# A hybrid decoder block on Trainium2: the seven-product scheme taken to the pooling and gate projections, with the stages in another order

## The chip, the cores and the metric

The kernel runs on one core of a Trainium2 chip. The metric is device time in microseconds, the median of several executions; lower is better. The engines are called as the profile calls them: PE (TensorE, the matmuls), PEld (its weight loads), ACT (ScalarE), DVE (VectorE), POOL (GpSimd) and SP (SyncE, which issues most loads).

## The reference, cut to what matters

528 tokens (16 learned meta tokens and 512 real ones) of width 1024 pass through one block:

```python
hn = rmsnorm(h, norm1_g)
q, k, v, glr, r, u, ga, gb = split(hn @ w_in)
o = rmsnorm(gla_chunked(q, k, v, log_a), gla_norm_g)      # 4 heads, chunked
y_a = (o * silu(r)) @ w_a
pooled = multiscale_pool(u)          # trailing means over 2, 4, 8, 16 tokens, minus the token
y_b = (einsum(pooled, w_pool_grp) * pool_scale) @ w_b
gate_a = sigmoid(ga + b_gates[:D]); gate_b = sigmoid(gb + b_gates[D:])
h = h + (gate_a * y_a + gate_b * y_b) @ w_o
hn = rmsnorm(h, norm2_g)
a, bv = split(causal_dwconv(hn @ w_up))
h = h + (silu(a) * bv) @ w_down
return rmsnorm(h, final_norm_g)[N_META:]
```

## The kernel before

**Layout.** Channels lie on the 128 partitions and tokens along the free axis, so a projection of 1024 channels is 8 output blocks m, each summed over 8 input blocks k. An f32 product is made of three matmuls on rounded halves: high by high, high by low, low by high. A tile therefore comes as a pair such as `xh`, `xl`: ACT copies the high part, DVE subtracts it for the low part (`split`, L248). Tokens are cut in two column parts, since a PSUM bank holds 512 numbers: `TAIL` is 258 + 256 columns (from token 14), `FULL` is 264 + 264. One block m is then 8 x 3 x 2 = 48 matmuls, and a pair of blocks 96.

**Order of the work.** The stages follow each other on PE as they are written: norm 1; k, q, the decay gates; v; the chunked linear attention with the r projections between its chunks (`gla_back`, `gla_front`, `proj_r`, L461-467); the head norms over the whole length (`head_squares`, `head_norm`, L469-506); then u, ga, a, gb, grp, b, o in that order, eight blocks each (grp is small); then the up projections with the down projections between them; and the final norm.

**The first part, k to o.** The weights of one block m come as a 512 KB chunk, loaded by SP three chunks and more ahead. `prep_chunk` (L124) makes the high part on ACT (L133) and the low part on DVE (L134), two chunks ahead. Each block's sum lands in a `psum` tile; DVE scales it by the first norm's factor (`scaled`, L262). The normalisation is thus applied behind the product: `xh`, `xl` hold x times the gain g1, without the factor `rstd1`.

**The pooling.** All of u is projected first (L511). The window sums of the four channel groups g are doubling trees of shifted adds: one add for g = 0, four for g = 3. They run on POOL (L520-537). While ga is projected, `pool_split` (L539) takes the mean minus the token on DVE (L544) and splits it into `pah`, `pal`. The gate ga is passed through a sigmoid (L555), and the result of a is multiplied by it as it is evicted (L560).

**The up stage** works in units, each of one pair of output blocks, from 1 MB of weights. `fetch` (L640) loads a unit's raw tile two and three units ahead. For the first three of its four blocks, `make_low` (L671) writes minus the raw weight, rounded, with ACT, and POOL then issues three accumulating transfers that add the weight from memory once more, which leaves the low part `gl`. `make_high` (L681) makes `gh` on ACT. Units 0 to 3 are plain, 96 matmuls. Units 4 to 21 (`up_fast`, L797) use a scheme of seven block products where a 2 x 2 product of blocks has eight. It needs sums of weight blocks (L704, splits `sh_..`, `sl_..`) and combinations of input blocks, which `cross` (L769) makes once per four input blocks, on an input that is already normalised. A group is 12 matmuls of 258 columns, a unit 7 groups, 84 matmuls. The bank x takes three groups, q two, v and y one each. ACT evicts x after its first group (L805), q after its first (L808), x after its second (L811) and its third (L817); DVE combines (L813-819). The next group into a bank waits until ACT has read the last. The work of the next units stands on the engines between these evictions, and each engine takes its instructions strictly in the order in which they stand.

**What sets the buffers.** The first part's pools are closed behind o (`first.close()`, L616); then the unit pools open (`rawp` 3, `gp` 2, `unitp` 14, `ssp` 2, `t3p` 4, eight PSUM banks). At the end of o, `h2` is made with its squares: DVE adds (L603), ACT makes `h2h` and the square (L604, L607), POOL adds the squares up (L611). The sum's split `n2h`, `n2l` (L613) feeds the norm matmuls (L758), which stand in the first up unit behind its first 48 matmuls.

Of the kernel before, what the change touches and what calls it, by code (L numbers as in the profile page):

```python
# [32 lines left out]
UCOLS = (((12, 270), (270, L)), ((10, 270), (270, L)), ((6, 268), (268, L)), FULL)  # L33
H0 = 12
HALF = ((H0, 270), (270, L))
HN = 258
PLAIN = 4
LAG = 3
CROSS = {(0, 1): 0, (1, 0): 1, (1, 1): 2, (2, 0): 3}
PARTS = ((0, 6), (6, 6), (12, 6), (18, 4))  # L40
# [14 lines left out]
for _name, _n in (  # L55
    ("k", 4), ("q", 4), ("v", 8), ("r", 8), ("u", 8), ("ga", 8), ("a", 8),
    ("gb", 8), ("grp", 2), ("b", 8), ("o", 8),
):
    ORDER[_name] = _at
    _at += _n  # L60
NCHUNK = _at

# [6 lines left out]
def hybrid_block(ctx: ExitStack, tc: tile.TileContext, xt, g1d, wts, wup, wdown, wglr, wgk, vecs, out):  # L69
# [4 lines left out]
    lastp = ctx.enter_context(tc.tile_pool(name="lastp", bufs=12))  # L74
    first = ctx.enter_context(ExitStack())
    firstp = first.enter_context(tc.tile_pool(name="firstp", bufs=16))
    midp = first.enter_context(tc.tile_pool(name="midp", bufs=8))
    wrawp = first.enter_context(tc.tile_pool(name="wrawp", bufs=3))
    whlp = first.enter_context(tc.tile_pool(name="whlp", bufs=3))
    work = first.enter_context(tc.tile_pool(name="work", bufs=5))  # L80
    constf = first.enter_context(tc.tile_pool(name="constf", bufs=1))
# [6 lines left out]
    class Pairs:  # L88
# [12 lines left out]
        "xh": lastp, "xl": lastp, "r": lastp, "gb": lastp, "h2": lastp, "h2h": lastp, "h2l": lastp,  # L101
        "kq_mid": midp, "kq_far": midp, "zh": midp, "zl": midp, "mh": midp, "ml": midp,
    }

    def big(name, dt=F32):
        return Pairs(name, HOME.get(name, firstp), dt)
# [76 lines left out]
    g1 = constf.tile([P, KT], F32, tag="g1", name="g1")  # L183
# [212 lines left out]
    o = big("o")  # L396
# [34 lines left out]
    def gla_back(s):  # L431
# [26 lines left out]
        for h in range(4):  # L458
            act.activation(o.pair(h)[:, :, c : c + w], heads[:, 2 * h : 2 * h + 2, 0:w], AF.Copy)
# [3 lines left out]
    for s in range(4):  # L463
        gla_back(s)
        gla_front(s + 1)
        proj_r(s + 1)
    gla_back(4)

    def head_norm(h):  # L469
        so = column_sums(f"nos{h}", osp[2 * h], osp[2 * h + 1], TAIL)  # L470
        ro = osq[2 * h][:, T0:]
        done, _ = rsqrt_mean(osq[2 * h], so, TAIL, 256, osq[2 * h + 1])
        for e in range(2):
            m = 2 * h + e
            dve.scalar_tensor_tensor(o[m][:, T0:], o[m][:, T0:], v1("glag", e), ro, ALU.mult, ALU.mult)
        return done

    osq = big("osq")
    osp = big("osp", F32R)

    def head_squares(h):
        act.activation(osq.pair(h)[:, :, T0:], o.pair(h)[:, :, T0:], AF.Square)
        t = osq[2 * h][:, T0:]
        dve.tensor_tensor(t, t, osq[2 * h + 1][:, T0:], ALU.add)
        split(osp[2 * h][:, T0:], osp[2 * h + 1][:, T0:], t)

    head_squares(0)
    proj_r(5)
    head_squares(1)
    proj_r(6)  # L490
    head_norm(0)
    head_squares(2)
    proj_r(7)
    head_norm(1)
    head_squares(3)

    u = big("u")

    def proj_u(m):
        acc = project(f"pu{m}", ORDER["u"] + m, xh, xl, UCOLS[m // 2])  # L500
        scaled(u[m], acc, UCOLS[m // 2])

    proj_u(0)
    head_norm(2)
    proj_u(1)
    done = head_norm(3)
    zh, zl = big("zh", F32R), big("zl", F32R)
    with tc.issue_after(done.ins):
        for m in range(8):
            act.activation(r[m][:, T0:], r[m][:, T0:], AF.Silu)  # L510
    for m in range(2, 8):  # L511
        proj_u(m)
        for i in (2 * m - 4, 2 * m - 3) if m < 6 else ():
            dve.tensor_tensor(o[i][:, T0:], o[i][:, T0:], r[i][:, T0:], ALU.mult)
            split(zh[i][:, T0:], zl[i][:, T0:], o[i][:, T0:])

    pts = [big("pt0"), big("pt1")]
    pah, pal = big("pah", F32R), big("pal", F32R)
    curs = []
    for g in range(4):  # L520
        cur = u.pair(g)
        need = T0
        starts = []
        for i in reversed(range(g + 1)):
            starts.append(need)
            need = max(0, need - (1 << i))
        starts = starts[::-1]
        for i in range(g + 1):
            d = 1 << i
            nxt = pts[g % 2].pair(2 * (g // 2) + i % 2)  # L530
            a = starts[i]
            if a < d:
                pool.tensor_copy(nxt[:, :, a:d], cur[:, :, a:d])
                a = d
            pool.tensor_tensor(nxt[:, :, a:], cur[:, :, a:], cur[:, :, a - d : L - d], ALU.add)  # L535
            cur = nxt
        curs.append(cur)

    def pool_split(g):  # L539
        cur = curs[g]  # L540
        if g == 3:
            pool.tensor_scalar(cur[:, :, T0 : T0 + 1], cur[:, :, T0 : T0 + 1], 16.0 / (T0 + 1), None, ALU.mult)
        ug = u.pair(g)[:, :, T0:]
        dve.scalar_tensor_tensor(ug, cur[:, :, T0:], 1.0 / (2 << g), ug, ALU.mult, ALU.subtract)  # L544
        split(pah.pair(g)[:, :, T0:], pal.pair(g)[:, :, T0:], ug)

    ga = big("ga")
    for m in range(8):
        acc = project(f"pga{m}", ORDER["ga"] + m, xh, xl, TAIL)
        done = scaled(ga[m], acc, TAIL)  # L550
        if 3 <= m < 7:
            with tc.issue_after(done.ins):
                pool_split(m - 3)
    for m in range(8):
        act.activation(ga[m][:, T0:], ga[m][:, T0:], AF.Sigmoid, bias=v1("bga", m))  # L555

    for m in range(8):
        acc = project(f"pa{m}", ORDER["a"] + m, zh, zl, TAIL)
        for src, c in parts_of(acc, TAIL):
            dve.tensor_tensor(ga[m][:, c], src, ga[m][:, c], ALU.mult)  # L560

    gb = big("gb")
    for m in range(8):
        acc = project(f"pgb{m}", ORDER["gb"] + m, xh, xl, TAIL)
        scaled(gb[m], acc, TAIL)
    pbh, pbl = big("pbh", F32R), big("pbl", F32R)
    for m in range(8):
        hi, lo = chunk(ORDER["grp"] + m // 4)
        acc = ps(f"pgrp{m}")
        g = m // 2  # L570
        products(
            acc,
            [(hi[:, 2 * (m % 4) + k], lo[:, 2 * (m % 4) + k], pah[2 * g + k], pal[2 * g + k]) for k in range(2)],
            TAIL,
        )
        for src, c in parts_of(acc, TAIL):
            act.activation(pbh[m][:, c], src, AF.Copy, scale=v1("pscale", m))
            dve.scalar_tensor_tensor(pbl[m][:, c], src, v1("pscale", m), f32(pbh[m][:, c]), ALU.mult, ALU.subtract)

    for m in range(8):  # L580
        last = act.activation(gb[m][:, T0:], gb[m][:, T0:], AF.Sigmoid, bias=v1("bgb", m))
    table(LOG_EXP, last)

    mh, ml = big("mh", F32R), big("ml", F32R)
    for m in range(8):
        acc = project(f"pb{m}", ORDER["b"] + m, pbh, pbl, TAIL)
        t = gb[m][:, T0:]
        for src, c in parts_of(acc, TAIL):
            dve.tensor_tensor(gb[m][:, c], src, gb[m][:, c], ALU.mult)
        dve.tensor_tensor(t, t, ga[m][:, T0:], ALU.add)  # L590
        split(mh[m][:, T0:], ml[m][:, T0:], t)

    h2 = big("h2")
    for i in range(4):
        pool.memset(h2.pair(i)[:, :, H0:T0], 0.0)
        sp.dma_start(h2.pair(i)[:, :, T0:], xt[2 * i : 2 * i + 2, :, T0:].rearrange("k p t -> p k t"))
    h2h, h2l = big("h2h", F32R), big("h2l", F32R)
    tot = None
    for m in range(8):
        acc = project(f"po2{m}", ORDER["o"] + m, mh, ml, TAIL)  # L600
        t = h2[m][:, T0:]
        for src, c in parts_of(acc, TAIL):
            dve.tensor_tensor(h2[m][:, c], src, h2[m][:, c], ALU.add)  # L603
        act.activation(h2h[m][:, T0:], t, AF.Copy, scale=v1("g2", m))  # L604
        dve.scalar_tensor_tensor(h2l[m][:, T0:], t, v1("g2", m), f32(h2h[m][:, T0:]), ALU.mult, ALU.subtract)
        sq = wk(f"n2_sq{m}", TW)
        act.activation(sq, t, AF.Square)  # L607
        if tot is None:
            tot = sq
        else:  # L610
            pool.tensor_tensor(tot, tot, sq, ALU.add)  # L611
    sh, sl = wk("n2h", L, F32R), wk("n2l", L, F32R)
    split(sh[:, T0:], sl[:, T0:], tot)  # L613
    rstd2 = const.tile([P, L], F32, tag="rstd", name="rstd2")
    n2t = wk("n2t")
    first.close()  # L616

    def phase(name, bufs):
# [116 lines left out]
    def up_plain(n, i):  # L735
# [4 lines left out]
        for c in range(2):  # L740
# [21 lines left out]
            if (i, c) in CROSS:  # L762
                cross(CROSS[i, c])
# [222 lines left out]
```

## Time and profile before

| quantity | value |
|---|---|
| runs | 842.43, 843.38, 843.58 us; median 843.38 |
| profiled execution | 842.5 us, of which the span is 840.2 |
| busy PE / DVE / ACT / POOL | 824.1 / 548.8 / 420.7 / 117.2 us |
| matmuls | 6357 in the records |
| stages on the chain | v 61.9 to 108.2; attention, r, head norms to 187.1; u to 234.5; ga to 280.2; a to 325.8; gb to 371.4; grp to 382.9; b to 428.8; o to 474.8; up and down to 823 |
| granted PE clock | 1.00 in the stages |
| memory traffic | 98.40 MB, mean 117 GB/s |

How to read it: the profile is of one execution, which lies 0.9 us under the median of the runs. Busy times are per engine and overlap. The chain is followed back from the last instruction, each piece to what released it, and is shown in order of time; an engine that is off the chain has slack somewhere. A row of a timeline or of the chain starts with its start and its length in us. A row of a group gives its busy us and the mean ns of one instruction, then the engine's idle time ahead of them and what ended it. Ends of matmuls are modelled, so a matmul's length is longer than its spacing; the spacing is what counts, and it is taken from a stage's length divided by its count.

### The profile page before, as it was taken

The numbers are of one execution on the slowest core, as the hardware profiler recorded it, in microseconds if no ns is written. First come the engines' busy times: TensorE is split into PE (matmuls) and PEld (weight loads), VectorE is DVE, ScalarE is ACT, GpSimd is POOL, SyncE is SP. The second block draws the span as 40 slices with busy tenths as digits, with TensorE's granted clock in tenths as the row PEclk, the third lists the DMA queues.
The fourth block names the chain that finished last, engine by engine and source line by source line (L and its number), as shares of the span: only waits on it lengthen the run. The fifth ranks groups of instructions, "written<-read, shape, count | busy, mean of one in ns | idle before, by whom it ended". The sixth has DMA issues, their size and how long they took to land.

```text
span 840.2 us, 15052 instructions
## 1 busy us (share of the span) xinstructions
PE 824.1 (98%) x6357; PEld 796.1 (95%) x6357; DVE 548.8 (65%) x833; ACT 420.7 (50%) x606; POOL 117.2 (14%) x117
## 2 busy tenths in 40 slices
PE   8999999999999999999999999999999999999994
PEld 7999999999999999999999999999989989999883
DVE  6677344469846433346556288999659975899845
ACT  7287243266334311344245256886547844686542
POOL 4000000001750000000014121220122110320021
PEclk9999999999999999999999999999999999999998
DMA  7423221022332333262268045886547645775102
GB/s 242 131 68 106 80 76 51 26 76 76 101 101 78 100 101 92 85 201 96 82 218 234 1 101 115 179 169 184 147 126 156 155 126 165 152 172 141 51 25 100
DMA packets 31170, 98.40 MB, mean 117 GB/s; under 512 B 3488, under 2 KB 6304, under 8 KB 28288
## 3 DMA queue, kind: packets, MB, share of 16 engines
q1 hardware_dynamic: 20368, 79.10, 29.2%
q0 software_dynamic: 9504, 17.31, 12.6%
q8 instruction: 49, 0.80, 0.4%
q10 hardware_dynamic: 1232, 1.05, 0.4%
q14 instruction: 17, 0.14, 0.0%
HBM read 95.35 MB, written 2.10 MB: 116 GB/s over the span
## 4 chain that ended last, share of the span: by engine, by line
PE 94%; DVE 2%; DMA 2%; ACT 1%; issue 0%; SPq 0%; DVEq 0%; POOL 0%; ACTq 0%
PE pd L847 12%; PE x L791 9%; PE q L791 6%; PE pu L150 6%; PE pv L150 6%; PE po L150 5%; PE pb L150 5%; PE pr L150 5%; PE pgb L150 5%; PE pga L150 5%; PE pa L150 5%; PE pup L750 4%; PE y L791 3%; PE v L791 3%; PE pq L150 3%; PE pe L847 2%
## 5 line engine op out<-in xcount | busy, mean ns | idle before, releaser
L133 ACT ACTIVATE whi<-wraw 128x1024 fp32r<-128x1024 f32 (+2 forms) x78 | 78.9, 1014 | 202.0 <-PE pa L150 36.4
L134 DVE TENSOR_TENSOR wlo<-wraw,whi 128x1024 fp32r<-128x1024 f32 (+2 forms) x78 | 94.8, 1218 | 13.1 <-ACT whi L133 7.3
L679 POOL DMA_DIRECT2D gl<-in_wup_dram x66 | 59.2, 1220 | 292.3 <-ACT gl L677 251.8
L847 PE MATMUL pd<-g,gh 128*128 128x512 f32 (+1 forms) x304 | 93.1, 387 | 0.0
L847 PEld LDWEIGHTS pd<-g,gh 128*128 128x128 f32 x304 | 56.5, 188 | 12.0
L704 DVE TENSOR_TENSOR raw<-raw 128x512 f32<-128x512 f32 x72 | 49.5, 688 | 19.3 <-ACT gh L687 10.3
L847 PE MATMUL pd<-g,gl 128*128 128x512 f32 (+1 forms) x152 | 58.8, 387 | 0.0
L687 ACT ACTIVATE gh<-raw 128x1536 fp32r<-128x1536 f32 x22 | 32.7, 1484 | 27.6 <-PE pd L847 24.3
L535 POOL TENSOR_TENSOR pt<-u 128x1028 f32<-128x1028 f32 (+3 forms) x4 | 14.0, 3498 | 191.9 <-ACT whi L133 179.0
L832 ACT ACTIVATE cv<-z,vec 128x512 f32<-128x512 f32 x44 | 34.2, 812 | 1.1 <-DVE cv L834 1.1
L847 PEld LDWEIGHTS pd<-g,gl 128*128 128x128 f32 x152 | 28.5, 188 | 6.1
L677 ACT ACTIVATE gl<-raw 128x1536 fp32r<-128x1536 f32 x22 | 32.5, 1477 | 2.8 <-PE pd L847 2.2
L833 DVE SCALAR_TENSOR_TENSOR cv<-z,vec,cv 128x512 f32<-128x512 f32 x44 | 32.2, 745 | 0.0
L834 DVE SCALAR_TENSOR_TENSOR cv<-z,vec,cv 128x512 f32<-128x512 f32 x44 | 32.2, 745 | 0.0
L870 DVE TENSOR_TENSOR h<-pd,h 128x512 f32<-128x512 f32 x24 | 16.5, 687 | 24.0 <-PE pd L847 24.0
L250 DVE TENSOR_TENSOR gl<-raw,gh 128x1536 fp32r<-128x1536 f32 (+1 forms) x16 | 26.0, 1622 | 6.6 <-ACT gh L249 6.4
L249 ACT ACTIVATE gh<-raw 128x1536 fp32r<-128x1536 f32 (+1 forms) x16 | 22.0, 1376 | 11.7 <-PE pd L847 9.2
L150 PE MATMUL pr<-xh,whi 128*128 128x258 f32 (+1 forms) x128 | 26.1, 285 | 0.0
L150 PE MATMUL pv<-xh,wlo 128*128 128x264 f32 x128 | 26.0, 284 | 0.0
L150 PE MATMUL pu<-xh,wlo 128*128 128x258 f32 (+3 forms) x128 | 25.9, 284 | 0.0
L150 PE MATMUL pv<-xl,whi 128*128 128x264 f32 x128 | 25.9, 284 | 0.0
L150 PE MATMUL pu<-xh,whi 128*128 128x258 f32 (+3 forms) x128 | 25.9, 284 | 0.0
(822 smaller groups left out, 2780.0 us busy)
## 6 DMA issues: line engine op xcount, KB each, us to landing
wraw<-in_wts_dram SPq DMA_DIRECT2D x72, 512.0 KB, 3.6
raw<-in_wup_dram SPq DMA_DIRECT2D x22, 1024.0 KB, 5.8
gl<-in_wup_dram POOLq DMA_DIRECT2D x66, 256.0 KB, 7.4
raw<-in_wdown_dram SPq DMA_DIRECT2D x12, 768.0 KB, 4.4
h<-in_xt_dram SPq DMA_DIRECT2D x4, 514.0 KB, 5.8
raw<-in_wdown_dram SPq DMA_DIRECT2D x4, 512.0 KB, 3.5
x<-in_xt_dram SPq DMA_DIRECT2D x7, 264.0 KB, 6.0
out_dram<-h ACTq DMA_DIRECT2D x4, 256.0 KB, 2.4
```

The lines of the kernel that those rows point to most:

```text
L133: act.activation(hi[:, a:b], t[:, a:b], AF.Copy)
L134: dve.tensor_tensor(lo[:, a:b], t[:, a:b], f32(hi[:, a:b]), ALU.subtract)
L150: pe.matmul(acc[:, s, : b - a], w, x[:, a:b], start=(i == 0 and w is wh and x is xh), stop=(i == n - 1 and last),)
L677: act.activation(lo, loaded[n][:, 0:3], AF.Copy, scale=-1.0)
L679: pool.dma_start(lo[:, b], wup[i, :, b], accum_op=ALU.add)
L687: act.activation(hi, loaded[n][:, 0:3], AF.Copy)
L704: dve.tensor_tensor(raw[:, dst], raw[:, dst], raw[:, x], ALU.add)
L750: pe.matmul(acc[:, 0 : b - a], w[p], q[k][:, a:b], start=k == 0 and e == 0, stop=k == KT - 1 and e == 2,)
L791: pe.matmul(acc[:, 0:HN], w[a][:, block, k], x[k][b][:, at], start=first and k == 0 and e == 0, stop=k == 3 and e == 2, skip_group_check=n ...
L832: act.activation(cv, z[:, c, META:], AF.Identity, scale=v1("cw2", m), bias=v1("cb", m))
L833: dve.scalar_tensor_tensor(cv, z[:, c, META - 1 : L - 1], v1("cw1", m), cv, ALU.mult, ALU.add)
L847: pe.matmul(acc, w[p][:, c, k], gated[k0 + k][q][:, a:b], start=k == 0 and e == 0, stop=k == nk - 1 and e == 2,)
```

## The change

- **Seven products.** u, ga and gb become units of one pair each, on the same machinery as the up stage, from a weight array of 1 MB units (`wsq`). Eleven of the twelve pairs (u1 to u3, ga0 to ga3, gb0 to gb3) use the seven-product scheme at 264 columns; the first pair of u stays plain. Its input is x times g1 times `rstd1`: x is loaded again (`load_x`), and `cross_x` makes the normalised blocks and their combinations during u0 and a0 to a2.
- **Plain units.** a, grp, b and o become plain units as well, with the same `gl`, `gh` machinery in place of the chunks. The unit pools open behind the last r block; `unitp` has 11 buffers.
- **Order.** u0, a0, a1, a2, u1, u2, a3, u3, ga0 to ga3, gb0 to gb2, grp, b0, gb3, b1 to b3, o0 to o3, then up as before.
- **Pooling.** The trees are issued on DVE (`pool_tree`): for u0 behind a2, for u1 behind u1, for u2 behind a3, for u3 behind u3, each with the mean and the split.
- **Gates.** a is evicted by ACT and kept, and multiplied by the gate when that is there.
- **Head norms** are taken chunk by chunk inside the attention loop, on 4 heads by 128 tokens at once.

The program has 138 matmuls fewer: 11 x 12, and 6 of the head norms.

The diff, cut to the parts spoken of:

```diff
-    pts = [big("pt0"), big("pt1")]
-            pool.tensor_tensor(nxt[:, :, a:], cur[:, :, a:], cur[:, :, a - d : L - d], ALU.add)
...
+    seq = [("plain", "u", 0)] + [("plain", "a", i) for i in range(3)]
+    seq += [("fast", "u", 1), ("fast", "u", 2), ("plain", "a", 3), ("fast", "u", 3)]
+    seq += [("fast", "ga", i) for i in range(4)] + [("fast", "gb", i) for i in range(3)]
+    seq += [("plain", "grp", 0), ("plain", "b", 0), ("fast", "gb", 3)]
+    seq += [("plain", "b", i) for i in range(1, 4)]
+    seq += [("plain", "o", i) for i in range(4)]
...
+    def fast(n, z, sides, cols):
+        direct, crossed = sides
+        g, sa, sb = weights(n)
...
+        seven(x, g, 2, direct, 2, w)
+        behind(act.activation(z11, x[:, n_], AF.Copy), make_high, n + 1)
+        make_sums(n + 1)
+        seven(q, sa, 0, crossed, 1, w)
+        act.activation(z22, q[:, n_], AF.Copy)
+        seven(v_, g, 0, crossed, 3, w)
+        seven(x, sa, 1, crossed, 2, w, False)
+        act.activation(z12, x[:, n_], AF.Copy)
...
+    def cross_x(i):
+        b = xb.pair(i)
+        for e in range(2):
+            k = 2 * i + e
+            dve.scalar_tensor_tensor(b[:, e], b[:, e], g1[:, k : k + 1], rstd1, ALU.mult, ALU.mult)
...
+    def pool_tree(g):
...
+            dve.tensor_tensor(nxt[:, :, a:], cur[:, :, a:], cur[:, :, a - d : L - d], ALU.add)
...
+        dve.scalar_tensor_tensor(ug, cur[:, :, T0:], 1.0 / (2 << g), ug, ALU.mult, ALU.subtract)
+        split(pah.pair(g)[:, :, T0:], pal.pair(g)[:, :, T0:], ug)
...
+        elif name == "a":
+            plain(n, i, zh, zl, TAIL, take_a, (CROSS_X, cross_x))
+            if i == 2:
+                pool_tree(0)
+            if i == 3:
+                pool_tree(2)
+        elif name == "u":
+            fast(n, u.pair(i), sides_x, FULL)
+            if i != 2:
+                pool_tree(i)
+        elif name == "ga":
+            z, _ = unit_gate(n, i, name)
+            y = ya.pair(i)[:, :, T0:]
+            dve.tensor_tensor(y, y, z[:, :, T0:], ALU.mult)
```

What stands on ACT around the second pooling split (`pah1`, of u1), before: the splits of pooling lie between the weight preparation of chunks that PE wants two chunks later.

```order
L133 ACTIVATE whi38_2915<-wraw38_2742 128x1024
L555 ACTIVATE ga1_2850<-ga1_2850,vec_96 128x514
L249 ACTIVATE pah0_2911<-u0_2189 128x2x514
L133 ACTIVATE whi39_2978<-wraw39_2799 128x1024
L555 ACTIVATE ga2_2970<-ga2_2970,vec_96 128x514
L249 ACTIVATE pah1_2974<-u1_2340 128x2x514
L133 ACTIVATE whi40_3040<-wraw40_2857 128x1024
```

After, on ACT from the end of u1 (unit 4) into u2 (unit 5). L710, L713, L716 and L722 are a unit's four evictions in order; `gh`, `gl` and `sh` are weights of units 5 to 7.

```order
L269 ACTIVATE sh_5a_2802<-raw5_2639 128x1024
L269 ACTIVATE sh_5b_2804<-raw5_2639 128x1024
L722 ACTIVATE u1_2779<-x4_2780 128x264
L597 ACTIVATE gl6_2892<-raw6_2764 128x1536
L269 ACTIVATE pah1_2902<-u1_2779 128x2x514
L710 ACTIVATE u2_2906<-x5_2907 128x264
L607 ACTIVATE gh6_2891<-raw6_2764 128x1536
L713 ACTIVATE u2_2906<-q5_2909 128x264
L607 ACTIVATE gh7_3010<-raw7_2889 128x1536
L269 ACTIVATE sh_6x_2925<-raw6_2764 128x512
L716 ACTIVATE u2_2906<-x5_2907 128x264
```

The split of the pooled u1 now stands between the last eviction of u1 and the first of u2, whose bank PE wants again within u2; before, nothing that PE waited for at once stood behind it. (L710 of u2 also waits for the low part, `pal1`, on DVE.) On PE the groups of u2 and of ga0 stand as x, q, v, y, x, q, x, where the other units have x, q, v, x, y, q, x (ga1 has most of y ahead too).

The tree of u3, before, on POOL, which had nothing else there:

```order
L533 COPY pt12_2673<-u3_2602 128x2
L535 TENSOR_TENSOR pt12_2673<-u3_2602 128x2x527
L535 TENSOR_TENSOR pt13_2676<-pt12_2673 128x2x526
L535 TENSOR_TENSOR pt12_2673<-pt13_2676 128x2x522
L535 TENSOR_TENSOR pt13_2676<-pt12_2673 128x2x514
L542 TENSOR_SCALAR pt13_2676<-pt13_2676 128x2
```

After, on DVE between u3 (unit 7) and ga0 (unit 8); `sl_8b` is a weight of ga0, L720 to L724 combine u3's products, L718 is the first of ga0.

```order
L720 TENSOR_TENSOR u3_3151<-q7_3154,u3_3151 128x264
L270 TENSOR_TENSOR sl_8b_3177<-raw8_3008,sh_8b_3176 128x1024
L723 TENSOR_TENSOR u3_3151<-u3_3151 128x264
L724 TENSOR_TENSOR u3_3151<-v7_3155,u3_3151 128x264
L766 COPY pt30_3269<-u3_3151 128x2
L768 TENSOR_TENSOR pt30_3269<-u3_3151 128x2x527
L768 TENSOR_TENSOR pt31_3272<-pt30_3269 128x2x526
L768 TENSOR_TENSOR pt30_3269<-pt31_3272 128x2x522
L768 TENSOR_TENSOR pt31_3272<-pt30_3269 128x2x514
L771 TENSOR_SCALAR pt31_3272<-pt31_3272 128x2
L773 SCALAR_TENSOR_TENSOR u3_3151<-pt31_3272,u3_3151 128x2x514
L270 TENSOR_TENSOR pal3_3279<-u3_3151,pah3_3278 128x2x514
```

The tree has moved from an engine without other work to the one that also prepares the weights, and its split (`pah3`) stands on ACT ahead of ga0's first eviction, as `pah1` does above.

At the end of o, before, POOL added the squares up one behind the other, with the last transfers of the low parts ahead of them:

```order
L611 TENSOR_TENSOR n2_sq0_4811<-n2_sq0_4811,n2_sq3_4996 128x514
L611 TENSOR_TENSOR n2_sq0_4811<-n2_sq0_4811,n2_sq4_5058 128x514
L611 TENSOR_TENSOR n2_sq0_4811<-n2_sq0_4811,n2_sq5_5118 128x514
L611 TENSOR_TENSOR n2_sq0_4811<-n2_sq0_4811,n2_sq6_5176 128x514
L611 TENSOR_TENSOR n2_sq0_4811<-n2_sq0_4811,n2_sq7_5232 128x514
```

After, on POOL at the same place; unit 24 is o3, 25 and 26 are up0 and up1:

```order
L599 DMA gl25_5285<-in_wsq_dram 128x512 x2
L836 TENSOR_TENSOR n2_sq0_4965<-n2_sq0_4965,n2_sq5_5279 128x514
L599 DMA gl25_5285<-in_wsq_dram 128x512
L836 TENSOR_TENSOR n2_sq0_4965<-n2_sq0_4965,n2_sq6_5351 128x514
L599 DMA gl26_5414<-in_wsq_dram 128x512 x2
L836 TENSOR_TENSOR n2_sq0_4965<-n2_sq0_4965,n2_sq7_5408 128x514
```

The adds now stand behind transfers of the next units' low parts, each of which is issued when ACT has made its copy; on ACT the copies `gh26` and `gl26` stand ahead of the last `h2h` and its square.

More of the change, by code (lines that the diff above doesn't have):

```diff
@@ L36 @@
 HN = 258
+FN = 264
 PLAIN = 4
@@ L465, in hybrid_block @@
         gla_front(s + 1)
+        hl = squares(s)
         proj_r(s + 1)
+        head_norm(s, hl)
     gla_back(4)
[L469 to L478, printed above, removed]
@@ L490, in hybrid_block @@
+    with tc.issue_after(done.ins):
+        for i in range(3):
+            gated_heads(i)
     proj_r(6)
-    head_norm(0)
-    head_squares(2)
     proj_r(7)
[L494 to L510, printed above, removed]
@@ L539, in pool_split @@
[L539 to L553, printed above, removed]
```

476 lines of the change are left out of this document (280 added, 196 removed).

## The prediction

> **What bounds the kernel now.** I read the page first: busy shares, then the chain of work that ended last.
>
> ```profile
> PE 824.1 (98%) x6357; PEld 796.1 (95%) x6357; DVE 548.8 (65%) x833; ACT 420.7 (50%) x606; POOL 117.2 (14%) x117
> ...
> PE 94%; DVE 2%; DMA 2%; ACT 1%; issue 0%; SPq 0%; DVEq 0%; POOL 0%; ACTq 0%
> ```
>
> TensorE is the bound. It works 98% of the span and carries 94% of the chain, so a matmul that goes shortens the span by its spacing, as long as nothing else comes late. I then read the chain piece by piece (start, length, what) over the stages that change.
>
> ```profile
> 61.94 46.31 PE pv L150 x384
> ...
> 187.12 5.81 PE pu L150 x48
> 192.93 0.47 PE nos L245 x4
> 193.40 5.80 PE pu L150 x48
> ...
> 199.70 34.83 PE pu L150 x288
> 234.54 45.65 PE pga L150 x384
> ...
> 325.79 45.65 PE pgb L150 x384
> ...
> 474.79 0.77 DVE h L603 x2
> 475.60 5.97 PE pup L750 x48
> ...
> 490.74 0.58 POOL gl L679
> 491.32 9.02 DMA gl<-in_wup_dram
> ...
> 583.00 16.55 PE pd L847 x72
> ```
>
> The pieces join without a gap from v to the end of o. The one hole is 0.8 us at 474.79, where the first up matmul wants a bank that the last eviction of o still holds.
>
> **What the matmuls give back.** A pair of ga or gb is 96 matmuls: 45.65 / 4 = 11.41 us. A pair of u takes (5.81 + 5.80 + 34.83) / 4 = 11.61. The new fast pair has 84 matmuls of 264 columns; v shows that width: 46.31 / 384 = 0.1206 us, so 84 x 0.1206 = 10.13. Eight gate pairs gain 8 x 1.28 = 10.25, u1 to u3 gain 3 x 1.48 = 4.45, and u0, plain on 258 columns, gains 0.15: 14.85 us. The program bears the count out: 138 matmuls fewer, 132 of them 11 x 12, the other 6 from the head norms. Those go from 16 short ones (four groups like the 0.47 shown, 1.9 us) to 8 of 512 columns at 16.55 / 72 = 0.23 and two tiny ones, about 2.0: 0.1 dearer. In the new order the first up pair takes a free bank, so the hole of about 0.85 us goes too. PE alone: -15.6.
>
> **Does another engine become the bound?** Two windows (length; busy PE, PEld, DVE, ACT, POOL; clock; DMA):
>
> ```profile
> 475.60:522.00 46.40, 46.31 (x388) 46.11 (x389) 35.64 (x59) 24.54 (x27) 9.25 (x10) 1.00 0.44 98
> 522.00:583.00 61.00, 61.00 (x507) 60.85 (x507) 58.20 (x92) 49.37 (x70) 13.25 (x15) 1.00 0.76 173
> 108.00:187.00 79.00, 79.00 (x684) 79.00 (x683) 40.59 (x63) 33.52 (x54) 0.00 (x0) 1.00 0.18 55
> ```
>
> In the second the same scheme already runs, with DVE at 95%, and PE does not stop. A gate unit carries no convolution, so it is lighter. The GLA stage (third row) has half of DVE and ACT free for the chunkwise norms; I take 0 for it, at worst 0.5 in each of four chunks. What decides is order, so I read the up stage's timeline around the end of one unit, where x ends at 532.28.
>
> ```profile
> 532.28 1.06 ACT L249 ACTIVATE sh_5b<-raw 128x1024 fp32r<-128x1024 f32 x1 [0.49 <-PE x L791]
> ...
> 533.51 1.48 ACT L677 ACTIVATE gl<-raw 128x1536 fp32r<-128x1536 f32 x1
> 534.88 0.38 ACT L805 ACTIVATE z<-x 128x258 f32<-128x258 f32 x1
> 535.15 1.49 ACT L687 ACTIVATE gh<-raw 128x1536 fp32r<-128x1536 f32 x1
> 536.52 0.38 ACT L808 ACTIVATE z<-q 128x258 f32<-128x258 f32 x1
> ```
>
> ```profile
> 533.37 1.23 DVE L250 TENSOR_TENSOR sl_5b<-raw,sh_5b 128x1024 fp32r<-128x1024 f32 x1
> 534.51 0.42 DVE L818 TENSOR_TENSOR z<-z 128x258 f32<-128x258 f32 x1
> 534.85 0.75 DVE L834 SCALAR_TENSOR_TENSOR cv<-z,vec,cv 128x512 f32<-128x512 f32 x1
> ```
>
> Here the next unit's first eviction (L805) starts 2.6 us after the old unit ends. TensorE wants it done before its next group into that bank: after three groups of 1.45, at 4.3, as a rule, and after four, at 5.8, in u2 and ga0, where the changed program has y ahead of it. So there are some 3 us of slack.
>
> **The pooling trees.** They move from POOL to DVE, straight behind u1 and u3, and their split (pah) stands on ACT ahead of the next unit's first eviction (L710). The rows give count, busy us and mean ns.
>
> ```profile
> L544 DVE SCALAR_TENSOR_TENSOR u<-pt,u 128x1028 f32<-128x1028 f32 x4 | 4.9, 1220 | 0.0
> ```
>
> ```profile
> L555 ACT ACTIVATE ga<-ga,vec 128x514 f32<-128x514 f32 x8 | 5.8, 727 | 0.0
> ...
> L249 ACT ACTIVATE pah<-u 128x1028 fp32r<-128x1028 f32 x4 | 4.3, 1066 | 1.6 <-DVE u L544 1.6
> ```
>
> Behind u1, counted from its end: sl_5b starts at 1.09, its follower at 2.23 (1.14 from start to start), the two corrections 0.34 apart, so DVE is free at 2.9. Two adds and the scaled difference, each 1.14: 6.4. pah, 1.07: 7.5. L710 of u2 also waits for pal, 1.23 as sl_5b: 8.8, and takes 0.38: 9.2. TensorE has stood since 5.8: **3.4 us**. Then gh6 lies ahead of L713 (0.27 + 1.37 by the rows above, 0.2 more wait), and gh7 and sh_6x ahead of L716 (0.7 more). u2: 4.3. Behind u3 the tree has four adds: free at 2.9, four adds and a tiny copy 4.7, difference 1.14, pah 1.07, L710 0.38, hand-overs: 10.4, less 5.8 = 4.6, and 0.2 behind gh9. ga0: 4.8. The bounds are 3.4 and 4.6 if ACT catches up at once, and 5.5 each if the shifted adds are slower than 1.14. The trees of u0 and u2 run beside a plain unit, whose evictions wait for nothing of them: 0.
>
> **The clock behind such a hole.** Nothing in mid-kernel shows one. The end does:
>
> ```profile
> 829.06 0.70 PE L900 MATMUL n3s<-sq,ones 128*128 128x256 f32 x2 [0.87 <-ACT sq L899]
> ```
>
> ```profile
> 833.00:833.50 0.50, 0.00 (x0) 0.00 (x0) 0.47 (x2) 0.00 (x0) 0.00 (x0) 0.87 1.03 332
> 833.50:834.00 0.50, 0.00 (x0) 0.00 (x0) 0.47 (x2) 0.00 (x0) 0.18 (x1) 0.50 0.98 354
> ```
>
> TensorE ends at 829.76 and the clock falls to half at about 833.37 (0.87 of that half microsecond's average), 3.6 us later. How long it then stays slow is seen at the start of the kernel:
>
> ```profile
> 1.39 4.02 PE L181 MATMUL heat<-warm 128*128 128x512 bf16 x9 [1.39 <-POOL warm L178]
> ...
> 6.53 0.65 PE L150 MATMUL pk<-xh,wlo 128*128 128x264 f32 x2
> 6.96 0.59 PE L150 MATMUL pk<-xl,whi 128*128 128x264 f32 x2
> 7.39 0.41 PE L150 MATMUL pk<-xh,wlo 128*128 128x264 f32 x2
> 7.63 0.53 PE L150 MATMUL pk<-xh,whi 128*128 128x264 f32 x3
> ```
>
> Two matmuls take 0.43 us up to 7.4 and 0.24 behind it: half speed for 6 us of work from 1.39 on, 3 us lost. ga0's hole of 4.6 is over 3.6, u2's of 3.4 is under it. I charge ga0 between 0 and 3, take 1.3 (some of the loss falls into the waits behind it), and u2 nothing.
>
> The Trainium skill, "TensorE: Matmul & The Clock Gate", Part 1, says that an idle window of about 3.4 us halves the clock and that about 3.4 us of work brings it back, in windows that run free. The 3.6 us at the end agree; the start shows a longer return. By that rule both holes could cost 1.7 us each (an estimate from it), 2.1 more than in my sum.
>
> **The small waits.** The pieces that TensorE multiplies with last, gl, come by accumulating transfers:
>
> ```profile
> gl<-in_wup_dram POOLq DMA_DIRECT2D x66, 256.0 KB, 7.4
> ...
> h<-in_xt_dram SPq DMA_DIRECT2D x4, 514.0 KB, 5.8
> ```
>
> - u0: DVE's first lattice waits for xb (loaded by SP, 5.8 us to landing, once older tiles give up their room), and the next unit's splits stand behind it: between 0 and one split, 1.2, take 0.4.
> - a1, a2, u1: the lattice of the normalised input holds up ACT's copies and so the gl transfers. The plain up units have the same lattice, the chain has a 9.02 us landing there, and PE was busy 46.31 of 46.40 all the same: 0.1. The upper end is a pair of splits, 2 x 1.07, in each; take 0.4 each, 1.2.
> - ga1 to gb3: ACT has gh and gl (2 x 1.48), two splits (2 x 1.06), four evictions (4 x 0.38) and two sigmoids (2 x 0.73, L555): 8.1 us for 10.13 of matmuls. One table load of sigmoids comes in too. 0 to 3, take 0.5.
> - grp, b, o as units: gl is made only when unit n-2 ends; two copies 2.8, POOL's issue 0.58, landing 7.4 make 10.8 against 11.4; with 9.02 it is 1.0 late. Take 0.8 for all, bounds 0 and 8.
> - up0: the last squares are now followed by the norm matmuls without the old hole:
>
> ```profile
> 478.96 0.69 DVE L250 TENSOR_TENSOR n2l<-n_sq,n2h 128x514 fp32r<-128x514 f32 x1 [1.87 <-ACT n2h L249]
> ```
>
> n2l was there at 479.65, 4.9 us after o ended. TensorE now wants it at 5.97. gh26 and gl26 (2.75 by the rows above, against 0.8 of eviction) stand ahead of the last h2h: 2.0 later, so 6.9, and POOL's two transfer issues may add 0.6: 0.9 to 1.5, take 1.2.
>
> **Sum.** 0.4 + 1.2 + 4.3 + 4.8 + 0.5 + 0.8 + 1.2 + 1.3 = 14.5 of new waits against 15.6: -1.1. The profiled execution took 842.5 (span 840.2 and 2.3 around it), so 841.4 there; the median of the runs, 843.38, lies 0.9 above it, so **842.3 us**. A measurement of this kernel can tell about 0.2%, 1.7 us, from no change: faster is below 841.7, slower above 845.1.
>
> **Rivals.**
> - *The holes don't open* (DVE and ACT ahead of my count, or the tree early enough): u2 and ga0 cost at most 1 together and the clock holds. 842.5 - 15.6 + 1 + 4.1 = 832.0, on the median 833; with the small waits at 0, 829. For it: in the up stage PE never waits for an eviction. Against it: the split is in order ahead of L710, and the tree cannot start before u1 ends. Chance 0.20.
> - *Slower, gl landings.* If most accumulating transfers land after 9 us rather than 7.4, each of a dozen plain units is 1.0 late instead of 0.1: +8, 850. It decides at 8.0 us. For it: the 9.02 above. Against it: it was seen where DMA works hard, share 0.44 to 0.76. Chance 0.15.
> - *Slower, the clock.* Both holes exceed 3.6 us and each is followed by 6 us of half speed: 2 x 3 - 1.3 = +4.7, 847. It decides at a hole of about 3.6 us; u2 stands at 3.4. For it: the fall at 833.4. Against it: part of the lost time would lie in the waits behind. Chance 0.15. (The Trainium skill's rule, same page and part, makes it the same case at a smaller price.)
> - *The change doesn't do what it says*: the count of matmuls excludes all but other faults, 0.02.
>
> **How the numbers follow.** The forecast's own case, 838.5 to 846, has 0.48: of it 0.23 lie under 841.7, 0.17 between, 0.08 above. Faster: 0.23 + 0.20 and 0.01 of the rest, 0.44. Slower: 0.08 + 0.15 + 0.12 and 0.01, 0.36; same: 0.17 + 0.03 of the clock's case, 0.20. The range reaches from the middle of the first rival to the second: 831 to 850; the likeliest case alone would be 838.5 to 846.
>
> **What would show it.** Right: fast units of 10.1 us; PE waiting for ACT (L710) 3 to 5 us in u2 and in ga0, with pah ahead of it on ACT; the clock below 1.00 behind ga0; 1 us at n2s. Wrong: no wait at L710 (first rival); PE waiting for DMA gl at the starts of plain units (second); matmuls at 0.24 us for 6 us behind u2 (third). If the new waits sum to less than 10 or more than 19, a term is mis-sized.

## The result: slower by 0.8%

The changed kernel took 849.94 us (median of four runs, 848.24 to 850.59) against 843.35 for the kernel before: a ratio of 1.0077, 95% interval 1.006 to 1.0095. Measured a second time (c_after below) it took 848.48 against 842.88, 1.0065 (1.0051 to 1.0079). The profiled execution of the first took 848.24, its span 846.2, where my sum gave 841.4. So the median lies at the very end of the range that I gave (831 to 850), and the kernel became slower, which I thought less likely than faster.

### The profile after

The page's busy times and its chain:

```profile
PE 817.5 (97%) x6219; PEld 786.4 (93%) x6219; DVE 581.3 (69%) x878; ACT 490.4 (58%) x688; POOL 152.7 (18%) x180
...
PE 82%; DMA 5%; DVE 5%; ACT 5%; issue 1%; POOL 0%; SPq 0%; DVEq 0%; ACTq 0%
```

The 138 matmuls are gone (6357 to 6219 records), and yet PE is busy only 6.6 us less. Its share of the chain falls from 94% to 82%. The chain also runs through other engines where TensorE has work meanwhile, so how long it really stood is seen in the list of what it waited for (in total, times, longest):

```profile
PE x L695 <- ACT ga L710: 5.3, 1, 5.3
PE x L695 <- ACT u L710: 3.9, 1, 3.9
...
PE x L695 <- DMA gl<-in_wsq_dram: 1.6, 2, 1.2
...
PE pp L663 <- DMA gl<-in_wsq_dram: 0.5, 1, 0.5
...
PE n2s L898 <- ACT n2hl L269: 0.4, 1, 0.4
```

The first two are the holes in ga0 and u2, each behind the eviction L710 and nowhere else. The chain through u2 (start, length, what), from the end of u1:

```profile
245.78 1.07 ACT sh_5b L269
...
246.87 1.23 DVE sl_5b L270
...
248.94 1.25 DVE pt L768
...
250.21 1.24 DVE pt L768
...
251.47 1.24 DVE u L773
...
252.73 1.07 ACT pah L269
...
253.82 1.24 DVE pal L270
...
255.15 0.40 ACT u L710
...
255.59 2.18 PE x L695 x12
257.77 2.52 PE q L695 x12
260.29 1.46 PE x L695 x12
```

This is the working of the prediction, step for step: the two adds and the mean, pah, pal, L710, and only then x. Counted from the start of sh_5b, 245.78, L710 ends at 9.8, where I had 9.2. A group of 12 takes 1.46 us, but the first two behind the hole are pieces of 2.18 and 2.52 (1.98 and 2.56 from start to start on the PE timeline). The windows show the clock in them (length; PE, PEld, DVE, ACT, POOL; granted clock):

```profile
250.00:256.00 6.00, 2.06 (x17) 1.84 (x16) 4.29 (x5) 1.91 (x3) 1.43 (x2) 1.00 0.95 220
256.00:258.00 2.00, 2.00 (x13) 2.00 (x13) 0.00 (x1) 2.00 (x3) 0.00 (x0) 0.65 0.96 175
258.00:262.00 4.00, 4.00 (x27) 4.00 (x27) 1.13 (x2) 1.58 (x4) 0.00 (x0) 0.75 0.30 66
```

The clock is still full at 256, when TensorE is at work again. It is half for about 1.4 of the next 2 us and 2.0 of the next 4: some 3.4 us in all, beginning behind the hole. In ga0 the tree is longer. The timeline of DVE, and of ACT, around it:

```profile
287.90 3.80 DVE L768 TENSOR_TENSOR pt<-pt 128x1052 f32<-128x1052 f32 x3
...
291.94 1.23 DVE L773 SCALAR_TENSOR_TENSOR u<-pt,u 128x1028 f32<-128x1028 f32 x1
```

```profile
293.21 1.06 ACT L269 ACTIVATE pah<-u 128x1028 fp32r<-128x1028 f32 x1 [7.11 <-DVE u L773]
294.17 0.37 ACT L710 ACTIVATE ga<-x 128x264 f32<-128x264 f32 x1
```

ACT stood 7.1 us in front of pah, with L710 ready behind it since its bank was full at about 284.7. That is how the hole comes about: an engine that takes its work in order, with an instruction at its head that waits.

**Where the 6 us came from.** Lengths between the first matmuls of the stretches, from the PE timelines of the two profiles:

| stretch | before | after | after, second profile |
|---|---|---|---|
| start to v | 61.8 | 62.5 | 62.1 |
| v | 46.3 | 46.9 | 46.9 |
| attention and r (1.0 of head norms moved in) | 78.9 | 80.0 | 80.0 |
| u to the second norm's matmuls | 294.4 | 294.0 | 295.5 |
| to the first fast up unit | 40.7 | 41.3 | 41.2 |
| to the first down part | 60.8 | 62.3 | 60.7 |
| to the final norm's matmuls | 242.4 | 244.1 | 244.5 |

The stretch that holds the change came out about even: what its matmuls gave back, the holes and the clock took. With the 1.0 of head norms left out and the last 15 us of the kernel added (0.3 and 0.2 longer), the rest is longer by 5.5 us in the first profile and 3.7 in the second, in stages where no other instruction of PE was altered. In the last stretch of the first profile TensorE waits once, 0.8 us, where the kernel before waits 0.7: its matmuls stand further apart.

### The profile page after: what moved, and what is told of

The parts are those of the page before. It is cut to its first block, busy times and chain, and to the rows that moved or that the text cites. A ratio compares the mean times of both kernels' runs of the same rounds, so it can differ in the third digit from the quotient of the medians.

```text
span 846.2 us, 15000 instructions
## 1 busy us (share of the span) xinstructions
PE 817.5 (97%) x6219; PEld 786.4 (93%) x6219; DVE 581.3 (69%) x878; ACT 490.4 (58%) x688; POOL 152.7 (18%) x180
## 4 chain that ended last, share of the span: by engine, by line
PE 82%; DMA 5%; DVE 5%; ACT 5%; issue 1%; POOL 0%; SPq 0%; DVEq 0%; ACTq 0%
PE pp L663 22%; PE pd L946 12%; PE x L695 11%; PE q L695 8%; PE pv L170 6%; PE pr L170 5%; DMA gl<-in_wsq_dram 5%; PE y L695 4%; PE v L695 4%; PE pq L170 3%; PE pe L946 2%; PE pk L170 1%; ACT gl L597 1%; PE po L468 1%; DVE pt L768 1%
## 5 line engine op out<-in xcount | busy, mean ns | idle before, releaser
L599 POOL DMA_DIRECT2D gl<-in_wsq_dram x141 | 127.4, 1214 | 561.1 <-ACT gl L597 489.1
L607 ACT ACTIVATE gh<-raw 128x1536 fp32r<-128x1536 f32 x47 | 69.8, 1485 | 63.9 <-PE pd L946 24.8
L624 DVE TENSOR_TENSOR raw<-raw 128x512 f32<-128x512 f32 x116 | 79.8, 688 | 30.0 <-ACT gh L607 17.6
L597 ACT ACTIVATE gl<-raw 128x1536 fp32r<-128x1536 f32 x47 | 69.4, 1477 | 13.5 <-PE pp L663 8.0
L153 ACT ACTIVATE whi<-wraw 128x1024 fp32r<-128x1024 f32 (+2 forms) x28 | 25.9, 933 | 52.5 <-PE pv L170 25.8
L154 DVE TENSOR_TENSOR wlo<-wraw,whi 128x1024 fp32r<-128x1024 f32 (+2 forms) x28 | 30.5, 1099 | 6.4 <-ACT whi L153 5.2
L170 PE MATMUL pv<-xh,whi 128*128 128x264 f32 x128 | 26.3, 287 | 0.0
L170 PE MATMUL pr<-xh,wlo 128*128 128x258 f32 (+1 forms) x128 | 25.8, 283 | 0.0
L170 PE MATMUL pr<-xl,whi 128*128 128x258 f32 (+1 forms) x128 | 25.6, 281 | 0.0
```

Source lines behind the costliest of these rows:

```text
L154: dve.tensor_tensor(lo[:, a:b], t[:, a:b], f32(hi[:, a:b]), ALU.subtract)
L170: pe.matmul(acc[:, s, : b - a], w, x[:, a:b], start=(i == 0 and w is wh and x is xh), stop=(i == n - 1 and last),)
L597: act.activation(lo, loaded[n][:, 0:3], AF.Copy, scale=-1.0)
L599: pool.dma_start(lo[:, b], wsq[UNIT[name] + i, :, b], accum_op=ALU.add)
L607: act.activation(hi, loaded[n][:, 0:3], AF.Copy)
L624: dve.tensor_tensor(raw[:, dst], raw[:, dst], raw[:, x], ALU.add)
```

## The experiments

**e1_pad and c_after: the places in memory, by 32 bytes; and the changed kernel again.** v and the fast units were slower per matmul than the row of before had it, and g1's move had shifted every later tile by 32 bytes.

```diff
-    g1 = const.tile([P, KT], F32, tag="g1", name="g1")
+    g1 = const.tile([P, 2 * KT], F32, tag="g1", name="g1")[:, 0:KT]
```

> The changed kernel with 32 bytes of padding behind g1 in the first pool, so that every later tile lies 32 bytes further on, at the same places modulo 64 as in the kernel before; no instruction differs. In the changed kernel v takes 46.9 us for the same 384 matmuls that took 46.3, a fast unit 10.29 us where 10.13 was worked out, and the up stage is some 1.4 us longer beside its waits. Theory (the places of the tiles in memory): v is back at 46.3 us, fast units at 10.13, the whole 4 us faster than the changed kernel, about 846. Rival (it is the change's traffic or the variation of runs): v stays at 46.9, fast units at 10.29, the time within 0.7 us of the changed kernel's 849.9.

> The changed kernel itself once more, beside the others of this call. Every theory expects about 850, with holes of 4 and 5.5 us in u2 and ga0; what is looked for is how far its waits for gl transfers change from run to run (2.1 us in its first profile, 1.3 and 2.8 in two variants), and by that how far its time spreads.

Measured: 847.39 with the padding, 1.0049 (1.0036 to 1.0062), and v stays as it was. The changed kernel itself gave 1.0077 and 1.0065, with intervals that overlap this one, so whether the padding took 0.2% off is not settled. The theory of 32 bytes falls with v. Its chain row:

```profile
61.71 46.94 PE pv L170 x384
```

The second profile of the changed kernel has the same two holes, 5.3 and 4.0 us, and 0.6 us of waits of x for gl, where the first had 1.6: the landings differ from run to run, the holes don't. The clock behind the holes differs too. Here it fell at 253.5 and at 294.5, before TensorE had resumed, and each time stayed at half for 6.8 us, twice as long as in the first profile. The windows over the fall and the return, and the chain's first groups behind each hole:

```profile
253.00:256.00 3.00, 0.52 (x2) 0.52 (x3) 1.66 (x2) 1.64 (x3) 0.00 (x0) 0.58 1.08 167
256.00:262.00 6.00, 6.00 (x35) 6.00 (x34) 1.12 (x2) 3.26 (x5) 0.00 (x0) 0.64 0.45 85
294.00:302.00 8.00, 6.87 (x33) 6.87 (x34) 5.91 (x8) 4.18 (x6) 0.00 (x0) 0.57 0.25 46
```

```profile
255.48 3.01 PE x L695 x12
258.49 2.34 PE q L695 x12
...
295.13 3.01 PE x L695 x12
298.14 2.64 PE q L695 x12
```

From start to start the groups lose 2.3 us behind u2's hole and 2.9 behind ga0's, 5.1 together, where the first profile lost 1.6 and 1.4. So the same two holes cost 3.0 us in one run and 5.1 in another.

**e2_fill: keep TensorE at work through the holes.**

```diff
+        if n in (5, 8):
+            spare = bank(f"spare{n}")
+            for _ in range({5: 28, 8: 40}[n]):
+                pe.matmul(spare[:, 0:w], g[0][:, 2, 0], direct[0][0][:, 2], start=True, stop=True)
         seven(x, sa, 1, crossed, 2, w, False)
```

> The changed kernel with 28 idle matmuls in u2 and 40 in ga0 (their result is read by nobody), placed just ahead of the group that waits for the eviction L710, so that TensorE works through most of the two holes. They take away no wait. Theory (the clock falls because of the holes): the clock stays at 1.00, the groups behind the holes take 1.46 us each, where they took 1.98 and 2.56 in u2 and 2.80 in ga0, and the time falls by about 3 us to 847. Rival (those groups are slow for the waits for L713 and L716 that stand behind gh): the groups stay as long and the time within 0.7 us of 849.9.

On PE the idle matmuls came to stand ahead of y, the group before the one that waits.

Measured: 845.79, 1.0031 (1.0019 to 1.0043), about 3 to 4 us under the changed kernel, what the clock cost in its two profiles being 3.0 and 5.1. The windows over u2 and over ga0 and ga1 (the changed kernel had 0.94 and 0.96 there):

```profile
235.50:262.00 26.50, 25.95 (x214) 25.73 (x213) 16.04 (x21) 15.02 (x21) 5.37 (x7) 1.00 0.73 173
283.00:325.00 42.00, 39.93 (x324) 39.30 (x323) 31.91 (x45) 27.02 (x36) 10.29 (x12) 1.00 0.67 144
```

The clock stays at 1.00, and the waits at L710 are now 0.6 and 0.5 us. ACT's order is the same, so L713 and L716 stand behind the same instructions as before; the groups x and q behind the holes take 1.46 to 1.57 us here, so the slow groups were the clock's. Sixty-eight useless matmuls made the kernel faster.

**e3_tree1: the tree of u1 behind u2.**

```diff
-            if i != 2:
-                pool_tree(i)
+            if i > 1:
+                pool_tree(2 * i - 3)
```

> The changed kernel with the pooling tree of u1, its mean and its split issued behind u2 in place of behind u1, so that they run beside the plain unit a3 with the tree of u2. Theory (what u2 waits for is this tree by way of pah and pal on ACT): u2 takes 10.3 us in place of 15.95, ga0 is unchanged at 17.1, time 849.9 - 5.7 = 844.2. Rival (the work comes up again): DVE has about 10 us of two trees beside the 11.4 us of a3, u3's sums come late and u3 waits 2 to 5 us in u2's place, time 847 to 850.

Measured: 843.63, 0.9994 (0.998 to 1.0008): 6 to 7 us less than the changed kernel by the two ratios, as the theory had it (5.7). The runs spread far, 840.5 to 849.49, and the profiled one is the slowest of them. In its waits the hole of u2 is gone, that of ga0 stands, and the plain units wait for gl:

```profile
PE x L695 <- ACT ga L710: 5.3, 1, 5.3
PE pp L663 <- DMA gl<-in_wsq_dram: 3.6, 3, 2.5
```

What this run lost is in unit a3, which has less time for its low parts to land now that u2 doesn't stand still: it took 18.05 us from start to start, where 11.39 is usual. Of the 6.7 more, 3.4 are two waits for gl (0.9 and 2.5), and the rest is the clock, which these shorter holes brought down as well, at 259.5 and for 6.8 us:

```profile
259.00:267.00 8.00, 6.78 (x34) 6.78 (x35) 4.25 (x5) 0.00 (x0) 1.11 (x2) 0.57 0.67 112
```

So the rival was right that lost time can come up again, but through late transfers and not through DVE's sums.

**e4_tree3: the tree of u3 in pieces.**

```diff
             if i != 2:
-                pool_tree(i)
...
+                pool_tree(3, later.append)
...
             dve.tensor_tensor(y, y, z[:, :, T0:], ALU.mult)
+            later.pop(0)()
```

> The changed kernel with the tree of u3 issued in pieces, one add behind each of ga0 to ga3, the mean behind gb0 and the split behind gb1. Theory: ga0 takes 10.3 us in place of 17.1, u2 is unchanged, time 849.9 - 6.8 = 843.1. Rival (DVE becomes the bound in the gate units, with 1.15 us more in each of six): each of ga1 to gb1 waits 0.5 to 1 us more, time 846 to 848.

Measured: 839.96, 0.9956 (0.994 to 0.9972): 9 to 10 us under the changed kernel by the two ratios. The hole of ga0 with its clock was 6.9 us in the first profile and 8.4 in the second. Of the two holes the wait list names that of u2 alone:

```profile
PE x L695 <- ACT u L710: 3.9, 1, 3.9
```

What is over, 1 to 3 us, I can't place; the waits for gl were few in the profiled run (1.2 us in all).

**e5_both: both trees put off.** The edits of e4_tree3, with the tree of u1 behind u2.

> The changed kernel with both trees put off: that of u1 behind u2, that of u3 in pieces behind ga0 to gb1. Theory (the two holes and the low clock behind them are 12.5 us of what was given back): both gone, no wait at L710 above 0.5 us, the clock 1.00 throughout, time 849.9 - 12.5 = 837.4, faster than the kernel before by 6 us. Rival (the work comes up again in the next units, as more waits for gl or for evictions): 842 to 846.

Measured: 834.78, 0.9908 (0.9894 to 0.9921), faster than the kernel before by 8 us, and some 14 under the changed kernel, more than the 12.5 of the theory, which had taken the clock's price from the first profile. No wait at L710 is left in the list, and the granted clock stays at 1.00 from the start of u to the last matmuls; these are the largest waits from u to the up stage:

```profile
PE pp L663 <- DMA gl<-in_wsq_dram: 0.8, 2, 0.5
PE x L695 <- DMA gl<-in_wsq_dram: 0.7, 1, 0.7
...
PE n2s L913 <- ACT n2hl L269: 0.4, 1, 0.4
```

**e9_split: the trees stay, only the splits are put off.** This parts the two things that stood between u1 and u2: DVE's work on the tree, and the place of the split, pah on ACT and pal on DVE.

```diff
+        if g % 2:
+            return ug
         split(pah.pair(g)[:, :, T0:], pal.pair(g)[:, :, T0:], ug)
...
             fast(n, u.pair(i), sides_x, FULL)
+            if i == 2:
+                split(pah.pair(1)[:, :, T0:], pal.pair(1)[:, :, T0:], ug)
             if i != 2:
-                pool_tree(i)
+                ug = pool_tree(i)
...
+            if i == 0:
+                split(pah.pair(3)[:, :, T0:], pal.pair(3)[:, :, T0:], ug)
```

> The changed kernel with the trees of u1 and u3 and their means left where they are on DVE, straight behind u1 and u3; only the two splits (pah on ACT, pal on DVE) are issued one unit later. Theory (it is the place of pah on ACT, ahead of L710, that holds TensorE, not the time that DVE spends on the tree): no wait at L710 above 0.5 us in u2 and ga0, u2 10.3 us and ga0 10.3 to 11.5, the time 837 to 840. Rival (DVE's 3.5 and 5.8 us of tree are the cost, in whatever order ACT stands): waits of 2 to 5 us for DVE in u2, ga0 or the unit behind each, time 844 to 848.

Measured: 837.38, 0.9928 (0.9902 to 0.9954), 11 to 13 us under the changed kernel. No wait at L710; u2 takes its usual length, 10.25. What DVE's load does cost is one wait in ga1, whose weight sums stand behind the tree of u3:

```profile
PE q L695 <- ACT sh_9a L269: 1.3, 1, 1.3
```

So of what the two holes and their clock cost (12.6 us in the first profile, 14.7 in the second) most came from the place of the two splits, and some 2 us, by which e5_both is faster still, from DVE's work. The edit moves pah and pal together and doesn't part them. In ga0 of the changed kernel L710 started right behind pah, at 294.17, so there pah alone held it.

**e7_pools, c_before, e8_best, e10_shift: why v is slower.** In e7_pools two groups of pools open in the old order, in e8_best (on top of e5_both) only the first part's; in e10_shift the kernel before gets the changed kernel's weight addresses.

```diff
-    constf = first.enter_context(tc.tile_pool(name="constf", bufs=1))
-    work = first.enter_context(tc.tile_pool(name="work", bufs=5))
     wrawp = first.enter_context(tc.tile_pool(name="wrawp", bufs=3))
     whlp = first.enter_context(tc.tile_pool(name="whlp", bufs=3))
+    work = first.enter_context(tc.tile_pool(name="work", bufs=5))
+    constf = first.enter_context(tc.tile_pool(name="constf", bufs=1))
...
-        phase(*a) for a in (("rawp", 3), ("gp", 2), ("unitp", 11), ("ssp", 2), ("t3p", 4))
+        phase(*a) for a in (("rawp", 3), ("gp", 2), ("ssp", 2), ("t3p", 4), ("unitp", 11))
```

> The changed kernel with two groups of pools opened in the order of the kernel before, so that the first part's weights lie where they lay before (185 to 205 thousand bytes; 198 to 219 thousand in the changed kernel) and the blocks d that TensorE multiplies with directly at 154 to 176 thousand (200 to 222 thousand). Same instructions. Theory (tiles high in memory are read more slowly): v falls from 46.93 to 46.3 us, a fast gate unit from 10.29 to 10.13, the groups y and the second q of the up stage from 1.446 and 1.459 to 1.436 and 1.446, the time by 2 to 3 us. Rival (v and the fast units are slower for another reason): v stays at 46.93 and the units at 10.29, the time within 1 us of the changed kernel in this call.

> The kernel before once more, with its profile, to see whether its lengths hold from run to run: v 46.3 us, the fast part of the up stage to the first down block 60.8, the last two down parts to the final norm as before. If v is 46.9 here, the 0.6 us are a matter of the run and not of the change.

> Both trees put off, and the first part's weight pools back at their old place in memory (only these; the up stage's pools stay as changed). Theory: the lengths of the two edits add up: v 46.3 us in place of 46.9, the rest as with both trees put off (834.8), so 834.2, about 1.0% faster than the kernel before. Rival (the gain at v is lost to other tiles that lie higher now): 834.8 or more, with v at 46.3 and another stage longer.

> The kernel before with its work and constant pools opened ahead of the weight pools, which puts the high and low weights of the first part where they lie in the changed kernel (198 to 223 thousand bytes, before 185 to 209). Same instructions. Theory (the place of these tiles alone makes v's matmuls slower): v takes 46.93 us in place of 46.31, the stages of 256 and 258 columns stay, the time rises by 0.6 to 1.2 us. Rival (another difference of the changed kernel): v stays at 46.31 and the time within 0.4 us of the kernel before.

Measured: the kernel before again 841.94 in one run; e7_pools 847.46, 1.0056 (1.0044 to 1.0069); e8_best 834.84, 0.9891 (0.9874 to 0.9908), not to be told from e5_both, though its v is short (46.32): the 0.6 us came up again elsewhere, as its rival had it; e10_shift 843.85, 1.0008 (0.9998 to 1.0018). The chain's row of v and a row of a down part in each. The changed kernel:

```profile
62.62 46.94 PE pv L170 x384
...
587.02 16.68 PE pd L946 x72
```

e7_pools:

```profile
61.70 46.31 PE pv L170 x384
586.48 16.68 PE pd L946 x72
```

The kernel before, again:

```profile
61.86 46.31 PE pv L150 x384
582.47 16.55 PE pd L847 x72
```

e10_shift:

```profile
62.00 46.33 PE pv L150 x384
584.10 16.55 PE pd L847 x72
```

v's length is no matter of the run: 46.31 in both profiles of the kernel before, 46.94 in the changed one and in every variant that keeps its pool order, 46.31 again as soon as the pools of the first part open in the old order. So in the changed kernel the order of the first part's pools sets it. But the weights' addresses alone don't: in e10_shift, by the sizes of the pools, they lie where the changed kernel has them, and v stays short. What else of the layout it is, stays open; tiles that other engines read and write at the same time have not been tried apart. In e7_pools a gate unit stays at 10.29 us; in the up stage the groups y and the second q come back to 1.44 and 1.45, while the second x goes from 1.43 to 1.46; and the time as a whole is that of the changed kernel. The theory that tiles high in memory are read more slowly is not borne out.

## Why the prediction was wrong

The mechanism was right, two holes behind L710 of about the size that was worked out, and the sign was not. Savings and new waits nearly cancel, and three steps of the sum failed: the stages that it left at zero, the clock behind the holes, and the price of a fast unit. By its own steps, for the profiled execution (841.4 in the sum, 848.24 measured):

- **Matmuls saved.** 138 fewer, as counted. The price of a fast unit, 84 x 0.1206 = 10.13 us, failed: two neighbouring units' second groups start 10.27 us apart,

```profile
323.42 1.48 PE q L695 x12
...
333.69 1.46 PE q L695 x12
```

  so the saving is some 1.5 us less over eleven units. The spacing came from a row of v in the kernel before, which in the changed kernel itself is 1.4% longer.
- **The holes.** By the starts of the groups on the PE timeline, y of u2 begins at 250.02 and x at 255.59, 5.57 for a group of 1.48: 4.1 against 4.3 in the sum (3.4 and the two small waits behind it, which did not show). In ga0 it is 287.62 to 294.60, 6.98 for 1.48: 5.5 against 4.8, since a dependent DVE step takes 1.26 from start to start and not 1.14. Together 0.5 more.
- **The clock behind them.** The term of the sum that was most mis-sized: I charged 1.3 for ga0 and nothing for u2, because u2's hole was to be 3.4 and the fall at the kernel's end came 3.6 us after the last matmul. It was 3.9 us long by the wait list, and the two groups behind it took 1.98 and 2.56 from start to start where 1.46 each is usual: 1.6. Behind ga0's they took 2.80 and 1.52: 1.4. Together 3.0, 1.7 more than charged, and e2_fill shows that they are the clock's. In the second profile they are 5.1, 3.8 more than charged. So u2's hole should not have been priced at nothing, and the 6 us of half speed at the kernel's start, 3 us lost, were a fair measure for the second profile (6.8 us of it behind each hole) and too long a one for the first (3.4). The Trainium skill, "TensorE: Matmul & The Clock Gate", Part 1, has about 3.4 us of work for the return. The first profile's 3.4 us at half agree, with 1.6 and 1.4 lost where an estimate from that page gave 1.7; the second's 6.8, with 2.3 and 2.9 lost, don't.
- **The small waits.** 4.1 us charged, 1.5 found between u and the second norm: the gl landings were seldom late there (0.5 at a plain unit, 0.4 in a gate unit) and n2s waited 0.6 for 1.2 charged. 2.6 less, and 3.3 less in the second profile, with 0.8 found. The rival of late landings did not come about, but for the one run of e3_tree1.
- **The stages left at zero.** This is the largest step that failed in the first profile: without it the sum would have come out level with the kernel before. The attention with its chunkwise norms was rightly near zero, 0.1 behind the moved matmuls. But start, v and everything from the second norm on were taken as unaltered, and they are 5.5 us longer, 3.7 in the second profile: v 0.6, the start 0.7 and 0.3, the last stretch 1.7 and 2.1, with down parts of 16.68 for 16.55, and waits for gl landings in the up stage that change from run to run (1.2 and 0.4). Of v it is shown that in the changed kernel the order of the first part's pools sets its length, not by what; the start has a wait of 1.7 us for wlo that the kernel before hasn't; why the other stages are longer stays open. No rival of mine had stages whose PE instructions stay.

Together 1.5 + 0.5 + 1.7 - 2.6 + 5.5 = 6.6 of the 6.8. In the second profile the same steps are 1.5, 0.5, 3.8, -3.3 and 3.7: there the clock counts for as much as the stages. That the new waits as a whole came to 14.1 and 15.5, against 14.5 in the sum, is luck: the clock was charged too little and the small waits too much. Of the rivals, the clock's came true in its place, u2 included, at a third of its 4.7 us in the first profile and four fifths in the second; the first one, that the holes don't open, is excluded by both. With the trees put off, e5_both is 8 us faster than the kernel before, where the matmuls alone would give 15.6: 1.5 of the rest is the price of the fast unit; the longer stages and the waits for gl are in the remainder, which was not taken apart.

## What to carry to other kernels

Price a move by the instruction that will stand behind it: a split of 1 us, put ahead of an eviction on an engine that works in order, cost the chain of work in front of it, not 1 us, and moving that split by one unit gave nearly all of it back. A hole on TensorE of 4 us cost 1.6 to 2.7 us more than itself, in the groups behind it, and one profile is not enough to tell how much. And where savings and costs nearly cancel, the stages that stay need a price too: v became 1.4% longer and a down part 0.8% without a change to their instructions.

## What the runs showed of the hardware

- Behind a hole the granted clock stood at half for 3.4 us or for 6.8, and for no other length: 3.4 in four cases (both holes of the first profile, ga0 in e1_pad, u2 in e7_pools) and 6.8 in seven (both of the second profile and of e3_tree1, u2 in e1_pad and in e4_tree3, ga0 in e7_pools). The groups behind u2's and ga0's holes lost 1.4 to 1.6 us in the one case and 2.3 to 2.9 in the other.
- The clock fell 2 to 5 us after TensorE's last matmul ahead of the hole. In u2 of the first profile that was 1.0 us after it had resumed (0.65 and 0.75 granted in the windows shown), so a hole can be paid for later than one looks for it. In e3_tree1 waits of 0.9 and 2.5 us in one unit were enough.
- Filling most of two holes with useless matmuls kept the clock at 1.00 and took 3 to 4 us off the time.
- The same 384 matmuls of v took 46.31 or 46.94 us, in the changed kernel by the order in which the pools were opened; 32 bytes of shift did nothing (46.94), nor did the weights' addresses alone (46.33).
